# A two-layer diffusion backbone: where the first feed-forward's gate vectors are fetched and multiplied

## The chip, the cores and the metric

The kernel runs on one core of one Trainium2 chip. The metric is the device time of one execution in microseconds (us). A core has a matrix engine (TensorE, written PE in the profile; its weight loads are PEld), a vector engine (VectorE, DVE), a scalar engine (ScalarE, ACT), a general one (GpSimd, POOL) and SyncE (SP), which here only issues DMAs. Matrix products are written to PSUM, which the kernel splits into eight banks of 128 x 512 floats: four "g", three "m" and one "v".

## What is computed

The reference runs two layers over 256 latent and 256 context tokens of width 1024. Layer 0 has a mixer of two kinds of scanned heads (GLA and mLSTM), layer 1 a Mamba-2 mixer; each is followed by a feed-forward with a depthwise convolution. Each half of a layer is modulated by vectors made from the conditioning vector `c` (and `c_ctx` for the context tokens):

```python
mod_l = (jax.nn.silu(c) @ mod_w[layer] + mod_b[layer])[:, None, :]
sh1l, sc1l, g1l, sh2l, sc2l, g2l = jnp.split(mod_l, 6, axis=-1)
...
xl = xl + g1l * yl                                   # the mixer's residual
hl = modulate(xl, norm_ffn_g[layer], sh2l, sc2l)     # norm, scale, shift
xl = xl + g2l * conv_ffn(hl, ...)                    # the feed-forward's residual
```

The products with `mod_w` (1024 x 6144 for each layer) have two useful rows each, but 25 MB of weights per layer. The last of the six vectors, `g2`, is the gate of the feed-forward.

## The kernel before

All activations lie transposed: `xT[k]` holds 128 features by 512 tokens (256 context, then 256 latent). Weights come from HBM in raw tiles of 1 MB (16 blocks of 128 x 128), and each half tile is split into a rounded part `wh` (ACT, L173) and a rest `wl` (DVE or POOL, L174), so that three fast matmuls (L185 to L187, helper `mm3`) replace one exact one. `Stream` does this one unit of eight blocks ahead; raw tiles lie in two buffers of the pool `rawp` (the feed-forward's up weights in two of their own, `ur`), split ones in four.

A product with `mod_w` is cut in chunks of 512 columns. `mod_chunk(l, j)` makes chunk j (0 to 11) of layer l: it loads 2 MB, runs eight exact fp32 matmuls (16 records on L244; four at a time lie side by side in the array, each 32 columns wide), copies the result to SBUF (ACT, L261), transposes it (PE, L264) and sums and biases it into `comps[l][j // 2]` (DVE, L268 to L272, helper `mod_out`). Chunks 10 and 11 are the gate `g2`, which layer 0 uses first in the feed-forward's residual. Chunk (1, 2) is half of the scale that layer 1's first norm uses.

Chunks run as fillers in other work. `Stream` has a list `fill`; whenever it loads a new raw tile it takes one element and calls it. `fill1[:-1]` is given to the first feed-forward's up weights from raw tile 2 on, so that each further tile takes a chunk; these use the pool `rawp` for their weights and the single "v" bank (`vps`) for result and transposes. The down weights of that feed-forward use `rawp`, too.

The order around the change in the program text: in `even_mixer` the four mLSTM heads (`head(0)` to `head(3)`), the output gates (`gates`), then `finish(0)` to `finish(3)`, each of which normalizes a head and writes two operands of the out-projection (`hh`, `hl`; square on ACT at L729, transposes L737, rounding L738, rest L739). Chunk (0, 10) stands ahead of `finish(0)` and chunk (0, 11) ahead of `finish(3)`; their weights use the four buffers "b4" of the mixer's pool `sp`, in loads of 512 KB. The out-projection follows: four column blocks at once, then four one after the other, each with its residual (L334) and a square that is summed for the norm (L286, L288; `Norm.add`). The norm: column sums by PE (L132), a reciprocal root in small DVE operations (L112 to L123), a spread over the partitions by four PE transposes (L140), a copy (L141), then for each of eight tiles DVE (L315), ACT (L321) and DVE (L323). Chunk (1, 2) stands between the spread and these tiles. The feed-forward (`conv_ffn`) makes up products for pairs j of column blocks (`project(j)`), convolves them on DVE (L798) and multiplies them down in two halves of 11 pairs. In the last pair of a half, `project(10)`, the second product goes to the "v" bank.

Program order is not the order on an engine. The tile framework plans each engine's queue ahead of time from estimated durations, and places waits by tile: so out-projection matmuls stand between those of the heads, and a chunk's matmuls between those of other products. Buffers of one name are given out in turn as they come free.

Of the kernel before, what the change touches and what calls it, by code (L numbers as in the profile page):

```python
# [9 lines left out]
F32 = mybir.dt.float32  # L10
# [6 lines left out]
P = 128  # L17
D = 1024
KD = 8
# [32 lines left out]
def block_kernel(ctx: ExitStack, tc: tile.TileContext, A: dict, out: bass.AP):  # L52
    nc = tc.nc
    PSUM = bass.MemoryType.PSUM
    v, s, g, te = nc.vector, nc.scalar, nc.gpsimd, nc.tensor
# [8 lines left out]
    rawp = ctx.enter_context(tc.tile_pool(name="rawp", bufs=2))  # L64
# [9 lines left out]
    def nm(b):  # L74
        _u[0] += 1
        return f"{b}_{_u[0]}"
# [149 lines left out]
    spad = cp.tile([P, KD, 32], F32, tag="spad", name="spad")  # L226
# [5 lines left out]
    ident = load(A["ident"], [P, P])  # L232
    comps = [[cp.tile([P, KD, 2], F32, tag=f"mod{l}_{i}", name=f"mod{l}_{i}") for i in range(6)] for l in range(2)]

    def mod_chunk(l, j, pool=rawp, psa=vps, tag="raw", n=2, bufs=None):

        ps = psa()
        w = KD // n
        for i in range(n):
            raw = pool.tile([P, w * 512], F32, tag=tag, name=nm("rawm"), bufs=bufs)  # L240
            nc.sync.dma_start(out=raw, in_=A["modw"][l, j, :, i * w * 512:(i + 1) * w * 512])
            for kk in range(w):
                k = i * w + kk
                te.matmul(out=ps[32 * (k % 4):32 * (k % 4) + 32, :], lhsT=spad[:, k, :], rhs=raw[:, kk * 512:(kk + 1) * 512],  # L244
                          start=k < 4, stop=k >= 4)
        mod_out(l, 4 * j, 4, ps, psa)

    def mod_part(q, pool, psa):

# [8 lines left out]
    def mod_out(l, c, n, ps, psa):  # L258

        ev = t2((P, n * P))  # L260
        s.copy(out=ev, in_=ps)  # L261
        pt = psa()[:, :n * P].rearrange("p (a b) -> p a b", b=P)
        for a in range(n):
            te.transpose(pt[:, a, :], ev[:, a * P:(a + 1) * P], ident)  # L264
        col = lambda name, o: pc(name, o, n).unsqueeze(2).to_broadcast([P, n, 2])
        i, k = c // KD, c % KD
        dst = comps[l][i][:, k:k + n, :]
        v.tensor_reduce(out=dst, in_=pt.rearrange("p a (q c) -> p a c q", q=4)[:, :, 0:2, :], axis=AX.X, op=ALU.add)  # L268
        v.tensor_tensor(out=dst, in0=dst, in1=col("modb", l * 48 + c), op=ALU.add)
        if i in (1, 4):  # L270

            v.scalar_tensor_tensor(out=dst, in0=dst, scalar=1.0, in1=col("nmg" if i == 1 else "nfg", l * 8 + k), op0=ALU.add, op1=ALU.mult)  # L272
# [33 lines left out]
    def norm_mod(l, comp_sh, comp_sc, segs, r, between=lambda k, acts: None, tiles=None):  # L306
        c0, c1 = segs[0][1], segs[-1][2]
        hs = [] if tiles is None else tiles
        sh, sc = comps[l][comp_sh], comps[l][comp_sc]
        acts = lambda k: hs[k]  # L310
        for k in range(KD):
            between(k, acts)
            y = t2()
            for ci, a, b in segs:
                v.scalar_tensor_tensor(out=y[:, a:b], in0=xT[k][:, a:b], scalar=sc[:, k, ci:ci + 1], in1=r[:, a - c0:b - c0],  # L315
                                       op0=ALU.mult, op1=ALU.mult)
            if tiles is None:
                hs.append(htiles(k))
            h_, l_ = hs[k]
            for ci, a, b in segs:  # L320
                s.activation(out=h_[:, a:b], in_=y[:, a:b], func=AF.Identity, bias=sh[:, k, ci:ci + 1])  # L321
            for ci, a, b in segs:
                v.scalar_tensor_tensor(out=l_[:, a:b], in0=y[:, a:b], scalar=sh[:, k, ci:ci + 1], in1=h_[:, a:b].bitcast(F32),  # L323
                                       op0=ALU.add, op1=ALU.subtract)
        return acts
# [18 lines left out]
    E = Ctx()  # L344
# [11 lines left out]
    with tc.tile_pool(name="stp", bufs=6) as stp:  # L356
        warm(10, ones)
        nrm = Norm(0, T)
# [17 lines left out]

        acts = norm_mod(0, 0, 1, SEGS, r, start)
    fill0 = [lambda j=j: mod_chunk(0, j) for j in (4, 5, 8, 9, 6, 7)]
    fill1 = [lambda j=j: mod_chunk(1, j) for j in (3, 0, 1, 4, 5, 8, 9, 6, 7, 11)]
    E.fill0, E.W0 = fill0, W0  # L380
    nrm = Norm(0, T)
    with ExitStack() as st:
        even_mixer(E, st, acts, pss0, nrm.add)
    for k in range(KD):
        dump(f"x1_{k}", xT[k])
    r = nrm.row()
    mod_chunk(1, 2, rawp, mps)
    acts = norm_mod(0, 3, 4, SEGS, r)
    with ExitStack() as st:
        hs, nrms = [], [Norm(a, b) for _, a, b in SEGS]  # L390

        def then(m, sgs):
            for sg in sgs:
                nrms[sg[0]].add(m)
                if m == KD - 1:
                    hs[:] = hs or [htiles(k) for k in range(KD)]
                    norm_mod(1, 0, 1, (sg,), nrms[sg[0]].row(), tiles=hs)

        conv_ffn(E, st, acts, fill1[:-1], then)
# [14 lines left out]
def even_mixer(E, st, acts, pss0, then):  # L414
# [343 lines left out]
    head(2)  # L758
    head(3)
    gates()  # L760
    E.mod_chunk(0, 10, sp, E.vps, "b4", 4, 4)
    finish(0)
    finish(1)
    finish(2)
    E.mod_chunk(0, 11, sp, E.vps, "b4", 4, 4)
    finish(3)
    for k in range(8):
        dump(f"m{k}", hh[k].bitcast(F32))
    WO = E.Stream(A["wout0"], 64)
# [4 lines left out]
    for m in range(4, KD):  # L774
        E.residual(0, 2, m, E.gemm_f(WO, 8 * m, KD, oa), SEGS)
        then(m)


class Conv:
# [586 lines left out]
```

## Time and profile before

| | |
|---|---|
| median of three runs | 1285.78 us (1279.78, 1285.78, 1286.11) |
| the profiled execution | 1282.09 us, of which the span of its instructions 1280.3 us |
| busy: PE, DVE, ACT, POOL | 96%, 72%, 46%, 33% of the span |
| chain that ended last | PE 75%, DVE 10%, issue 4%, DMA 4%, ACT 4%, POOL 2% |
| mean granted TensorE clock | 0.987 of full speed |
| L244, the chunks' matmuls | vps x288 and mps x32 records (20 chunks of 16) |

How to read it: a busy share is an average over stages with different limits. The chain is followed back from the last instruction, at each step to what released it. In a timeline a row has the start in us, the time it took, engine, line, operation, the tile written and the tiles read, and how many instructions of one kind in a row it stands for; in brackets the idle time of that engine before it and what ended it. Matmuls are pipelined: the time that one costs is the distance from start to start, not its duration. Tile names are the program's, with the buffer number left out.

### The profile page before, as it was taken

To read this page: it belongs to the slowest core of one execution; us is meant where nothing else is said; L and a number is where in the kernel's file an instruction comes from. 1 tells how busy PE (TensorE), PEld (TensorE's weight loads), DVE (VectorE), ACT (ScalarE), POOL (GpSimd) and SP (SyncE) were. 2 spreads that over 40 slices of the span, in tenths; PEclk is the share of its full clock that TensorE was granted. 3 is DMA by queue.
4 is the path that set the end of the run, shared out by engine and by line. 5 is a ranking of instruction groups with operands and counts; after the bars stand their busy time and mean duration, and the time that the engine had idled before them with its cause. 6 is when DMAs were issued, how large, how long until landed. Compare 5 with 4: busy or idle time off the path is not lost.

```text
span 1280.3 us, 18746 instructions
## 1 busy us (share of the span) xinstructions
PE 1227.8 (96%) x7094; PEld 1003.9 (78%) x7094; DVE 926.0 (72%) x2061; ACT 594.4 (46%) x937; POOL 428.8 (33%) x249
## 2 busy tenths in 40 slices
PE   7989999999999999999999999999999998999995
PEld 5657787876867777888888897888888897899994
DVE  4483889487658776227785478888888956989995
ACT  4463345344344333223443346666666645555543
POOL 0100000000225565326666000032222224999974
PEclk8999999999999999999999999999999998999998
DMA  9557202334536564222211225453544376555521
GB/s 372 200 187 234 107 22 78 129 107 165 172 130 263 202 259 166 99 99 99 99 66 66 99 75 147 142 168 124 165 131 125 108 270 218 193 172 191 178 91 61
DMA packets 40106, 191.45 MB, mean 150 GB/s; under 512 B 4608, under 2 KB 10568, under 8 KB 21072
## 3 DMA queue, kind: packets, MB, share of 16 engines
q1 hardware_dynamic: 36512, 185.48, 41.6%
q10 hardware_dynamic: 3504, 4.77, 1.2%
q8 instruction: 56, 0.92, 0.3%
q14 instruction: 34, 0.28, 0.1%
HBM read 189.03 MB, written 1.20 MB: 149 GB/s over the span
## 4 chain that ended last, share of the span: by engine, by line
PE 75%; DVE 10%; issue 4%; DMA 4%; ACT 4%; POOL 2%; SPq 0%; DVEq 0%; ACTq 0%; POOLq 0%
PE gps L185 12%; PE gps L186 12%; PE gps L187 12%; PE mps L185 6%; PE mps L187 6%; PE mps L186 6%; PE vps L244 3%; PE gps L932 1%; PE vps L1174 1%; PE gps L933 1%; PE gps L931 1%; POOL wl L174 1%; PE gps L220 1%; PE gps L222 1%; PE gps L221 1%
## 5 line engine op out<-in xcount | busy, mean ns | idle before, releaser
L174 POOL TENSOR_TENSOR wl<-raw,wh 128x1024 fp32r<-128x1024 f32 x122 | 293.6, 2415 | 495.7 <-ACT wh L173 459.4
L173 ACT ACTIVATE wh<-raw 128x1024 fp32r<-128x1024 f32 x226 | 237.4, 1054 | 170.8 <-PE gps L187 99.6
L185 PE MATMUL gps<-hh,wh 128*128 128x512 f32 (+1 forms) x824 | 290.8, 354 | 6.7 <-ACT hh L321 4.9
L186 PE MATMUL gps<-hh,wl 128*128 128x512 f32 (+1 forms) x824 | 289.6, 352 | 1.1 <-DVE wl L174 1.1
L187 PE MATMUL gps<-hl,wh 128*128 128x512 f32 (+1 forms) x824 | 290.2, 353 | 0.0
L798 DVE SCALAR_TENSOR_TENSOR y<-mps,fcw,y 128x255 f32<-128x255 f32 (+3 forms) x592 | 247.5, 433 | 51.7 <-ACT y L792 37.5
L185 PEld LDWEIGHTS gps<-hh,wh 128*128 128x128 f32 x824 | 155.6, 189 | 41.7 <-issue 12.5
L174 DVE TENSOR_TENSOR wl<-raw,wh 128x1024 fp32r<-128x1024 f32 x104 | 127.6, 1234 | 79.6 <-ACT wh L173 79.4
L185 PE MATMUL mps<-hh,wh 128*128 128x256 f32 (+1 forms) x544 | 178.2, 328 | 0.0
L187 PE MATMUL mps<-hl,wh 128*128 128x256 f32 (+1 forms) x544 | 176.5, 325 | 1.6 <-DVE hl L323 1.6
L186 PE MATMUL mps<-hh,wl 128*128 128x256 f32 (+1 forms) x544 | 177.0, 325 | 0.0
L186 PEld LDWEIGHTS gps<-hh,wl 128*128 128x128 f32 x824 | 156.1, 189 | 23.2 <-issue 3.2
L187 PEld LDWEIGHTS gps<-hl,wh 128*128 128x128 f32 x824 | 156.0, 190 | 20.8 <-issue 1.7
L185 PEld LDWEIGHTS mps<-hh,wh 128*128 128x128 f32 x544 | 105.4, 194 | 16.9 <-issue 6.7
L187 PEld LDWEIGHTS mps<-hl,wh 128*128 128x128 f32 x544 | 105.2, 194 | 9.2 <-DVE hl L323 1.8
L186 PEld LDWEIGHTS mps<-hh,wl 128*128 128x128 f32 x544 | 105.6, 194 | 7.8
L798 DVE SCALAR_TENSOR_TENSOR y<-gps,fcw,y 128x189 f32<-128x189 f32 (+3 forms) x180 | 77.7, 438 | 22.0 <-ACT y L792 18.2
L792 ACT ACTIVATE y<-mps,fcw 128x256 f32<-128x256 f32 (+1 forms) x68 | 41.2, 637 | 91.5 <-PE mps L187 91.5
L185 PE MATMUL gps<-mh,wh 128*128 128x512 f32 (+1 forms) x198 | 73.5, 371 | 0.0
L187 PE MATMUL gps<-ml,wh 128*128 128x512 f32 (+1 forms) x198 | 73.4, 371 | 0.0
L186 PE MATMUL gps<-mh,wl 128*128 128x512 f32 (+1 forms) x198 | 73.4, 370 | 0.0
L334 DVE SCALAR_TENSOR_TENSOR x<-gps,mod,x 128x256 f32<-128x256 f32 x56 | 24.2, 478 | 42.0 <-PE gps L187 42.0
(292 smaller groups left out, 1894.0 us busy)
## 6 DMA issues: line engine op xcount, KB each, us to landing
raw<-in_up SPq DMA_DIRECT2D x42, 1024.0 KB, 4.9
rawm<-in_modw SPq DMA_DIRECT2D x36, 1024.0 KB, 6.6
raw<-in_win SPq DMA_DIRECT2D x32, 1024.0 KB, 5.4
raw<-in_dn SPq DMA_DIRECT2D x20, 1024.0 KB, 5.1
raw<-in_wout SPq DMA_DIRECT2D x10, 1024.0 KB, 5.6
rawm<-in_mods SPq DMA_DIRECT2D x8, 1024.0 KB, 14.5
R<-crd SPq DMA_DIRECT2D x32, 256.0 KB, 4.2
rawm<-in_modw SPq DMA_DIRECT2D x8, 512.0 KB, 5.0
```

Source lines behind the costliest of these rows:

```text
L173: s.activation(out=hi[:, :n], in_=rw, func=AF.Copy)
L174: self.eng(u).tensor_tensor(out=lo[:, :n], in0=rw, in1=hi[:, :n].bitcast(F32), op=ALU.subtract)
L185: te.matmul(out=ps, lhsT=lhi, rhs=rhi, start=first, stop=False)
L186: te.matmul(out=ps, lhsT=llo, rhs=rhi, start=False, stop=False)
L187: te.matmul(out=ps, lhsT=lhi, rhs=rlo, start=False, stop=last)
L220: te.matmul(out=ps, lhsT=ah[:, sl], rhs=hi[:, c:c + 512], start=k == 0, stop=False)
L221: te.matmul(out=ps, lhsT=ah[:, sl], rhs=lo[:, c:c + 512], start=False, stop=False)
L222: te.matmul(out=ps, lhsT=al[:, sl], rhs=hi[:, c:c + 512], start=False, stop=k == nk - 1)
L244: te.matmul(out=ps[32 * (k % 4):32 * (k % 4) + 32, :], lhsT=spad[:, k, :], rhs=raw[:, kk * 512:(kk + 1) * 512], start=k < 4, stop=k >= 4)
L334: v.scalar_tensor_tensor(out=xT[m][:, a:b], in0=ps[:, a - base:b - base], scalar=gt[:, m, ci:ci + 1], in1=xT[m][:, a:b], op0=ALU.mult, op1 ...
L792: self.E.s.activation(out=y, in_=ps, func=AF.Identity, scale=self.fcw[:, c + 4:c + 5], bias=self.fcw[:, c + 9:c + 10])
L798: self.E.v.scalar_tensor_tensor(out=o, in0=i, scalar=self.fcw[:, ti * 10 + wi:ti * 10 + wi + 1], in1=o, op0=ALU.mult, op1=ALU.add)
```

## The change

Chunks (0, 10) and (0, 11) are no longer made among the `finish` calls. `mod_chunk` is split into `mod_load` (buffers and DMAs), `mod_go` (matmuls) and the old `mod_out`. The loads now stand behind `finish(3)`, ahead of the out-projection's: (0, 10) in the four "b4" buffers as before, (0, 11) in the two "tok" buffers in which the mixer held its values, with 1 MB each. The matmuls stand behind the out-projection, in "g" banks; (0, 10) is finished there, while the copy, transposes and sums of (0, 11) are returned as a function and called behind `norm_mod`. Chunk (1, 2) leaves the norm and becomes the first element of `fill1`, all others move back by one.

```diff
--- before.py
+++ after.py
@@ -232,18 +232,25 @@
     ident = load(A["ident"], [P, P])
     comps = [[cp.tile([P, KD, 2], F32, tag=f"mod{l}_{i}", name=f"mod{l}_{i}") for i in range(6)] for l in range(2)]
 
+    def mod_load(l, j, pool=rawp, tag="raw", n=2, bufs=None):
+
+        w = KD // n * 512
+        for i in range(n):
+            raw = pool.tile([P, w], F32, tag=tag, name=nm("rawm"), bufs=bufs)
+            nc.sync.dma_start(out=raw, in_=A["modw"][l, j, :, i * w:(i + 1) * w])
+            yield raw
+
+    def mod_go(l, j, raws, psa):
+        ps = psa()
+        k = 0
+        for raw in raws:
+            for c in range(0, raw.shape[-1], 512):
+                te.matmul(out=ps[32 * (k % 4):32 * (k % 4) + 32, :], lhsT=spad[:, k, :], rhs=raw[:, c:c + 512], start=k < 4, stop=k >= 4)
+                k += 1
+        return lambda: mod_out(l, 4 * j, 4, ps, psa)
+
     def mod_chunk(l, j, pool=rawp, psa=vps, tag="raw", n=2, bufs=None):
-
-        ps = psa()
-        w = KD // n
-        for i in range(n):
-            raw = pool.tile([P, w * 512], F32, tag=tag, name=nm("rawm"), bufs=bufs)
-            nc.sync.dma_start(out=raw, in_=A["modw"][l, j, :, i * w * 512:(i + 1) * w * 512])
-            for kk in range(w):
-                k = i * w + kk
-                te.matmul(out=ps[32 * (k % 4):32 * (k % 4) + 32, :], lhsT=spad[:, k, :], rhs=raw[:, kk * 512:(kk + 1) * 512],
-                          start=k < 4, stop=k >= 4)
-        mod_out(l, 4 * j, 4, ps, psa)
+        mod_go(l, j, mod_load(l, j, pool, tag, n, bufs), psa)()
 
     def mod_part(q, pool, psa):
 
@@ -376,16 +383,16 @@
 
         acts = norm_mod(0, 0, 1, SEGS, r, start)
     fill0 = [lambda j=j: mod_chunk(0, j) for j in (4, 5, 8, 9, 6, 7)]
-    fill1 = [lambda j=j: mod_chunk(1, j) for j in (3, 0, 1, 4, 5, 8, 9, 6, 7, 11)]
+    fill1 = [lambda j=j: mod_chunk(1, j) for j in (2, 3, 0, 1, 4, 5, 8, 9, 6, 7, 11)]
     E.fill0, E.W0 = fill0, W0
     nrm = Norm(0, T)
     with ExitStack() as st:
-        even_mixer(E, st, acts, pss0, nrm.add)
+        rest = even_mixer(E, st, acts, pss0, nrm.add)
     for k in range(KD):
         dump(f"x1_{k}", xT[k])
     r = nrm.row()
-    mod_chunk(1, 2, rawp, mps)
     acts = norm_mod(0, 3, 4, SEGS, r)
+    rest()
     with ExitStack() as st:
         hs, nrms = [], [Norm(a, b) for _, a, b in SEGS]
 
@@ -758,12 +765,16 @@
     head(2)
     head(3)
     gates()
-    E.mod_chunk(0, 10, sp, E.vps, "b4", 4, 4)
     finish(0)
     finish(1)
     finish(2)
-    E.mod_chunk(0, 11, sp, E.vps, "b4", 4, 4)
     finish(3)
+
+    mods = [list(E.mod_load(0, 10, sp, "b4", 4, 4)), []]
+    for i in range(2):
+        raw = T_([P, 4, 516], "tok", bufs=2).rearrange("p a b -> p (a b)")[:, :2048]
+        nc.sync.dma_start(out=raw, in_=A["modw"][0, 11, :, i * 2048:(i + 1) * 2048])
+        mods[1].append(raw)
     for k in range(8):
         dump(f"m{k}", hh[k].bitcast(F32))
     WO = E.Stream(A["wout0"], 64)
@@ -774,6 +785,8 @@
     for m in range(4, KD):
         E.residual(0, 2, m, E.gemm_f(WO, 8 * m, KD, oa), SEGS)
         then(m)
+    E.mod_go(0, 10, mods[0], E.gps)()
+    return E.mod_go(0, 11, mods[1], E.gps)
 
 
 class Conv:
```

## Rows read from the trace of the kernel before

**Rows 1.** Busy us by stage: length, PE, PEld, DVE, ACT, POOL, clock, DMA

```profile
296.00:353.00 57.00, 55.85 (x270) 41.44 (x269) 38.63 (x99) 18.88 (x30) 7.25 (x3) 1.00 0.49 170
353.00:362.00 9.00, 6.22 (x43) 3.35 (x41) 5.07 (x21) 3.76 (x7) 2.36 (x1) 1.00 0.46 168
362.00:400.00 38.00, 38.00 (x178) 28.44 (x179) 25.39 (x61) 18.64 (x29) 12.99 (x6) 0.96 0.49 191
```

**Rows 2.** Timeline of PE at the mixer's end

```profile
296.30 1.06 PE L244 MATMUL vps<-rawm,spad 128*32 128x512 f32 x8
297.30 0.50 PE L185 MATMUL gps<-hh,wh 128*128 128x512 f32 x1
...
300.19 1.05 PE L244 MATMUL vps<-rawm,spad 128*32 128x512 f32 x4
302.40 1.05 PE L244 MATMUL vps<-rawm,spad 128*32 128x512 f32 x4 [1.15 <-DMA rawm<-in_modw]
...
304.41 0.60 PE L264 MATMUL vps<-c,t 128*128 128x128 f32 x4
304.77 0.48 PE L185 MATMUL gps<-hh,wh 128*128 128x512 f32 x1
```

**Rows 3.** Timeline of ACT, DVE and PE around finish(3)

```profile
312.84 0.62 ACT L729 ACTIVATE t<-qk 128x512 f32<-128x512 f32 x1
...
321.13 0.75 DVE L739 SCALAR_TENSOR_TENSOR hl<-mps,c,hh 128x512 fp32r<-128x512 f32 x1 [1.48 <-ACT hh L738]
...
328.63 0.39 PE L185 MATMUL gps<-hh,wh 128*128 128x512 f32 x1
```

**Rows 4.** Timeline of PE and DVE through the norm

```profile
352.89 0.39 PE L187 MATMUL gps<-hl,wh 128*128 128x512 f32 x1
...
354.10 1.04 PE L244 MATMUL mps<-rawm,spad 128*32 128x512 f32 x2
...
356.16 1.92 PE L244 MATMUL mps<-rawm,spad 128*32 128x512 f32 x14
...
358.51 0.16 DVE L123 SCALAR_TENSOR_TENSOR ry<-rw,ry 128x4 f32<-128x4 f32 x1
...
358.83 0.55 PE L264 MATMUL mps<-c,t 128*128 128x128 f32 x3 [0.75 <-ACT t L261]
359.21 0.60 PE L140 MATMUL vps<-c,ry 128*128 128x128 f32 x4
...
361.95 0.53 PE L185 MATMUL gps<-hh,wh 128*128 128x512 f32 x1 [2.03 <-ACT hh L321]
```

**Rows 5.** Busy us by stage: one stretch behind the norm

```profile
364.00:365.00 1.00, 1.00 (x4) 0.81 (x3) 1.00 (x4) 0.72 (x2) 0.00 (x0) 0.50 1.06 451
```

**Rows 6.** Timeline of PE, one chunk in the feed-forward

```profile
380.10 1.92 PE L244 MATMUL vps<-rawm,spad 128*32 128x512 f32 x16
```

**Rows 7.** Timeline around the last chunk and the down-projection's start

```profile
487.86 1.92 PE L244 MATMUL vps<-rawm,spad 128*32 128x512 f32 x16
...
488.98 0.33 SPq L159 DMA_DIRECT2D raw<-in_dn  x1
...
491.63 0.19 DVE L268 TENSOR_REDUCE mod<-vps 128x8 f32<-128x32 f32 x1
...
501.23 0.39 PE L185 MATMUL vps<-hh,wh 128*128 128x512 f32 x1
...
506.67 0.40 PE L185 MATMUL gps<-mh,wh 128*128 128x512 f32 x1
...
507.75 4.61 DVE L798 SCALAR_TENSOR_TENSOR y<-vps,fcw,y 128x255 f32<-128x255 f32 x10 [0.82 <-ACT y L792]
```

**Rows 8.** Page, groups (busy us, mean ns of one); DMA issues (us to landing)

```profile
L174 POOL TENSOR_TENSOR wl<-raw,wh 128x1024 fp32r<-128x1024 f32 x122 | 293.6, 2415 | 495.7 <-ACT wh L173 459.4
L173 ACT ACTIVATE wh<-raw 128x1024 fp32r<-128x1024 f32 x226 | 237.4, 1054 | 170.8 <-PE gps L187 99.6
...
raw<-in_dn SPq DMA_DIRECT2D x4, 512.0 KB, 5.8
```

## The prediction, made before the change was run

> **What bounds the kernel now.** I read the chain that ended last first (mostly TensorE, PE), then the table by stage, which says where PE is the limit [rows 1]: between 296 and 353 us (end of the first mixer, out-projection) PE is busy 55.85 of 57.00 us, in the feed-forward's first 38 us all 38, but in the 9 us between (the norm) only 6.22. So in the first and third stretch every PE instruction that is removed or added counts at its full price, as long as its operands are there; in the norm PE waits for a chain over VectorE (DVE) and ScalarE (ACT), and work put there is free as long as it doesn't stand in front of that chain. The change moves three products of one kind between these stages. I call them fills: 0/10 and 0/11 (gates of the first feed-forward) and 1/2 (a scale of the second layer). Last I read the timeline around each of them.
>
> **Part A: 0/10 and 0/11 leave the mixer's end.** A fill is 16 PE records on L244 and 4 transposes on L264. Fill 0/10 took PE from 296.30 to 297.30 (8 records), and from 300.19 to 303.40 (4 records, an idle 1.15 us for the weights, 4 records from 302.40, 1.0 us) [rows 2]: 1.00 + 3.21 us. Fill 0/11 comes in three such pieces without the wait, 3.0 us. The four transposes of each delay the next matmul from 304.41 to 304.77, 0.36 us. Sum: 4.21 + 3.00 + 0.72 = 7.9 us. It is all gained if the out-projection's matmuls can close up, and they can if their operands are ready. The last one, hl of finish(3), was ready at 321.13 + 0.75 = 321.88, and its twelve matmuls began at 328.63 [rows 3], 6.75 us of slack. If finish(3) didn't move at all, the gain would be 6.7 us, not 7.9. But it will move: its square waited until 312.84 [rows 3], on an ACT queue that also held the evacuations of both fills. I take 7.4 us (bounds 6.7 and 7.9).
>
> The eight loads of these weights become six and stay where they are in SP's queue; those of 0/11 now need "tok" buffers, free after the last head. The out-projection's last load stands behind them as before. I cost this at nothing: that load's blocks are used in the last quarter of the out-projection. If that cover were gone, the price would be one landing, about 6 us.
>
> **Part B: the norm.** The last out-projection matmul starts at 352.89 and the first feed-forward matmul at 361.95 [rows 4], 9.06 us. Now PE does fill 1/2 there; later it does 0/10 and 0/11. Fill 1/2 hardly cost anything: PE is in it until 356.16 + 1.92 = 358.08, and the chain (the reciprocal root on DVE) ends at 358.51 + 0.16 = 358.67. Only three of its transposes, which had waited for their ACT copy, stand ahead of the four that spread the root over the partitions; these start at 359.21 instead of 358.7, 0.5 us late. Two fills need 2 x (1.92 + 0.36) = 4.6 us of PE. There are 0.75 us idle before 358.83, 2.1 us idle between the spread's end (359.81) and 361.95, and the 2.4 us that 1/2 gives back: 5.3 us. It fits, if the order is right. Bounds: with all 32 records and the first four transposes ahead of the spread, PE comes to it at 356.16 + 30 x 0.12 + 0.55 = 360.3 [rows 4], 1.1 us later than now; two copies and small DVE operations of mod_out ahead of the chain's could add 0.9: +2.0 us. Below nothing: the spread 0.5 us early, and the clock. [...] Before it fell, PE had been idle for 2.1 us. If the second fill closes this, the clock may hold: -2.0 us in all. I take +0.3 us, nearest to the row of 1/2, which cost 0.5.
>
> [...] The rows show that the spread's transposes started 0.5 us after their operand, behind three that waited for a copy. [...]
>
> **Part C: 1/2 becomes a fill of the feed-forward.** fill1 gets one more element, so ten fills instead of nine run there, each in its turn. One costs 1.92 us [rows 6] and 0.36 us of transposes, 2.3 us of a full PE. And the last of them comes to another place. A fill is taken with every 16th block of the up weights; the tenth meets project(10), whose second product goes into the one vps bank (from 501.23) [rows 7], where fills are done too. The ninth held that bank from 487.86 until DVE had reduced it at 491.63 + 0.19, 4.0 us; so project(10)'s second half waits up to 4.0 - 2.3 = 1.7 us. The tenth also holds both "raw" buffers until it is multiplied, from 501.2 to 502.2 for the first. The down-projection's first load was issued at 488.98, right behind the ninth fill [rows 7]; now it goes at 502.3. Landing 5.8, ACT's rounding 1.05, GpSimd's rest 2.4 us [rows 8]: 511.6 us. The down-projection began at 506.67 [rows 7]; its new due time is 506.67 + 2.3 + 1.7 = 510.7, so 0.9 us are lost there. C lies between 2.3 us (the tenth is multiplied as soon as it lands, before its turn) and 2.3 + 1.7 + 0.9 = 4.9 us. I take 3.4, near the middle, as no row shows a fill in this place.
>
> **Sum.** -7.4 + 0.3 + 3.4 = -3.7 us. The profiled execution took 1282.09 us (span 1280.3); the change would make that 1278.4. The median of the three runs is 3.69 us (0.29%) higher, 1285.78, so the forecast stands at 1282.1. The bounds together are -7.9 - 2.0 + 2.3 = -7.6 and -6.7 + 2.0 + 4.9 = +0.2 us: 1278.2 to 1286.0.
>
> **Rivals.**
> 1. Both fills stand before the spread. For it: all of 1/2's records and three transposes did. Against: they were all that PE had to do. -7.4 + 2.0 + 3.4 = -2.0 us, 1283.8.
> 2. Faster: the clock holds through the norm, the spread loses its 0.5 us, the tenth fill is multiplied early. For it: PE's longest idle time in the norm gets work. Against: the clock fell in spite of 4 us of L244 shortly before. -7.6 us, 1278.2.
> 3. Slower: the tenth fill loses the vps bank. If project(10)'s second half takes the bank first, the fill waits until DVE has convolved that product, 507.75 + 4.61 = 512.4 us [rows 7]. Both raw buffers stay full, the down-projection's load goes at 513.4 and is split at 513.4 + 5.8 + 1.05 + 2.4 = 522.7, while PE has nothing else from 506.67 on: 16 us, and 0.5 us of the fill that isn't covered. It decides from the point where the fill's weights land later than project(10)'s first half ends, or where the planner ranks the product first. Against: the ninth's fill went ahead of its product. -7.4 + 0.3 + 16.5 = +9.4 us, 1295.2.
> 4. The weights of 0/10 and 0/11 now live until the norm, in space that the first up weights may be meant for. Then these wait for the fills, some 6 us after the last out-projection matmul; 9.25 us of landing and splitting [rows 8] make 15.3 instead of 9.06: B is +6.2, the sum +2.2 us, 1288.0. Against: the mixer frees far more space than these 33 KB of each partition.
> 5. The change doesn't do what it says: the planner multiplies both fills inside the out-projection, at 4.6 us of a full PE, and the norm gets its 0.5 us back. -7.4 + 4.6 - 0.5 + 3.4 = +0.1 us, 1285.9. Against: 1/2, which depends on nothing in the out-projection, began at 354.10, behind its last matmul [rows 4].
>
> **How the numbers follow.** Forecast 52%, rival 1 14%, rival 2 15%, rival 3 8%, rival 4 4%, rival 5 7%. The predicted time is the forecast's, 1282 us. The range must take in 1278.2 to 1286.0; the three runs shown differ by 6.3 us, so I widen it to 1276 and 1289, which leaves out rival 3 and a few per cent of the others. A measurement of this kernel can tell about 0.5% (6.4 us) from no change. Faster by more than that: rival 2 and the lower edge of the forecast, 0.23. Slower: rival 3 and the upper edge of rival 4, 0.10. Within: 0.67.
>
> **What would show it.** A: no L244 between 290 and 315, no idle time of PE there, and the last out-projection matmul at about 345.5. B: 32 records of L244 right behind it; from that matmul to the first of the feed-forward 9 us again (7 to 11); the clock 1.00 behind it, or not. C: ten fills after the norm, the last before or within project(10); the idle time ahead of the first down-projection matmul says which bound holds. The prediction is wrong if PE has gaps in the out-projection (then operands, not PE, were the limit), or if the down-projection starts more than 3 us behind project(10).

## The result, and the profile after

The changed kernel takes 1298.01 us (median of 4 runs), the kernel before in the same comparison 1282.97 us: a ratio of 1.0103 with a 95% interval of 1.0078 to 1.0129. By the ratio it is 13 us slower (by the medians 15) where 4 us faster were forecast, and outside the predicted range.

Where the time went can be read from the starts of the same VectorE instructions in the two profiled runs (1296.84 against 1282.09 us). After minus before:

| stretch of the kernel before | shift in it | forecast |
|---|---|---|
| up to 250 us | +0.7 | 0 |
| 250 to 262 us, mLSTM heads | +3.5 | 0 |
| 290 to 348 us, mixer's end (part A) | -8.9 | -7.4 |
| 348 to 440 us, norm and start of the feed-forward (part B) | +15.1 | +0.3 |
| 500 to 520 us, last fills (part C) | +3.9 | +3.4 |
| the rest | +0.3 | 0 |

A and C came with the forecast sign, each somewhat larger. Two stretches carry the error: B, and one in the heads of which the prediction had said nothing. First the table by stage (stretch, its length, busy time of each engine, granted clock, DMA share and rate):

```profile
core 0: us, PE busy (x) PEld busy (x) DVE busy (x) ACT busy (x) POOL busy (x), PEclk, DMA share, GB/s
296.00:347.00 51.00, 51.00 (x249) 42.32 (x248) 33.32 (x102) 17.56 (x32) 0.00 (x0) 1.00 0.32 113
347.00:357.00 10.00, 9.25 (x63) 4.65 (x61) 3.20 (x16) 1.22 (x2) 0.00 (x0) 1.00 0.01 2
357.00:385.00 28.00, 18.02 (x64) 12.53 (x64) 19.27 (x34) 12.38 (x23) 13.96 (x4) 0.76 0.56 207
```

The mixer's end is closed up: 51 of 51 us busy, against 55.85 of 57 [rows 1]. But in the 28 us behind the norm TensorE works for only 18, at a mean clock of 0.76; before, it was full there at 0.96 [rows 1]. GpSimd, idle until 357, works half of this time. TensorE's timeline through the norm:

```profile
348.27 1.05 PE L132 MATMUL vps<-ones,acc 128*128 128x128 f32 x8
351.32 1.92 PE L248 MATMUL gps<-rawm,spad 128*32 128x512 f32 x14
354.57 1.92 PE L248 MATMUL gps<-tok,spad 128*32 128x512 f32 x16
356.43 0.65 PE L140 MATMUL vps<-c,ry 128*128 128x128 f32 x4
357.75 1.92 PE L248 MATMUL vps<-rawm,spad 128*32 128x512 f32 x16 [0.67 <-ACT rstd L141]
362.62 0.92 PE L185 MATMUL mps<-hh,wh 128*128 128x512 f32 x2 [2.94 <-ACT wh L173]
365.12 0.80 PE L186 MATMUL mps<-hh,wl 128*128 128x512 f32 x1 [1.57 <-POOL wl L174]
377.64 0.80 PE L186 MATMUL mps<-hh,wl 128*128 128x512 f32 x1 [4.79 <-POOL wl L174]
```

Both fills (on L248 in this kernel) stand ahead of the spread (L140, at 356.43; the last out-projection matmul began at 348.04, so 8.38 us behind it, against 6.33 before [rows 4]); this is rival 1. Behind them even 1/2 is multiplied, first of the ten. Then TensorE waits for the up weights, which it did not do there before ([rows 4] show only a wait for hh): for wh from ScalarE, and twice for wl from GpSimd. SyncE's queue tells why they are late, in its timeline and in its list of waits (in total, times, longest):

```profile
356.56 0.33 SPq L159 DMA_DIRECT2D raw<-in_up  x1
```
```profile
SPq L159 <- PE gps L248: 25.6, 1, 25.6
```

The up weights' first load was issued at 356.56, right behind the last matmul of 0/11, after waiting 25.6 us for it; before, it was issued at 320.51. That is rival 4's wait. Its landing and the split of the weights (ScalarE's rounding and GpSimd's subtraction), which had been done inside the out-projection, now lie in and behind the norm (ACT and POOL, then two rows of the table by stage):

```profile
361.51 1.06 ACT L173 ACTIVATE wh<-raw 128x1024 fp32r<-128x1024 f32 x1 [1.95 <-DMA raw<-in_up]
362.70 4.88 POOL L174 TENSOR_TENSOR wl<-raw,wh 128x1024 fp32r<-128x1024 f32 x2 [310.92 <-DMA raw<-in_up]
371.02 9.09 POOL L174 TENSOR_TENSOR wl<-raw,wh 128x1024 fp32r<-128x1024 f32 x2 [3.44 <-ACT wh L173]
```
```profile
373.00:378.00 5.00, 0.36 (x1) 0.36 (x2) 4.87 (x8) 2.98 (x6) 5.00 (x2) 0.87 0.00 0
378.00:383.00 5.00, 5.00 (x15) 3.93 (x15) 0.00 (x0) 0.00 (x0) 2.10 (x1) 0.50 0.36 106
```

The third subtraction, from 371.02 to the matmul that it lets go at 377.64, took 6.6 us; one takes 2.4 us elsewhere [rows 8]. Behind the idle time that it makes, the clock is 0.50 for 5 us. (It is at 0.50 from 363 to 368 too, behind the wait for wh.)

The second loss, in the heads. SyncE's and VectorE's timelines, and the table by stage:

```profile
246.93 0.33 SPq L776 DMA_DIRECT2D tok<-in_modw  x1
```
```profile
254.47 0.35 DVE L705 SCALAR_TENSOR_TENSOR b<-b,RQT,c_trineg 128x128 f32<-128x128 f32 x1 [2.89 <-DMA b<-prd]
```
```profile
246.00:250.00 4.00, 3.61 (x25) 3.04 (x24) 3.52 (x15) 0.60 (x1) 0.00 (x0) 1.00 0.76 244
250.00:254.00 4.00, 4.00 (x20) 3.24 (x18) 1.58 (x8) 1.85 (x3) 0.00 (x0) 1.00 0.65 250
254.00:258.00 4.00, 1.71 (x10) 1.29 (x9) 3.53 (x10) 1.96 (x3) 0.00 (x0) 0.90 0.00 0
258.00:262.00 4.00, 4.00 (x14) 3.25 (x13) 3.06 (x7) 1.17 (x4) 0.00 (x0) 0.68 0.38 131
```

The first half of 0/11 is loaded at 246.93 already: one of the two "tok" buffers is free as soon as the linear attention has read gv. While this 1 MB arrives (250 GB/s), VectorE waits 2.89 us for the broadcast of a head's gates on ScalarE's queue; TensorE runs dry (busy 1.71 of 4 us), and its clock falls to 0.68 in the 4 us behind that.

### The profile page after: what moved, and what is told of

Its sections match the earlier page's. It is cut to its first block, busy times and chain, and to the rows that moved or that the text cites. A ratio compares the mean times of both kernels' runs of the same rounds, so it can differ in the third digit from the quotient of the medians.

```text
span 1294.7 us, 18744 instructions
## 1 busy us (share of the span) xinstructions
PE 1231.0 (95%) x7094; PEld 1007.9 (78%) x7094; DVE 924.1 (71%) x2061; ACT 594.2 (46%) x937; POOL 433.1 (33%) x249
## 4 chain that ended last, share of the span: by engine, by line
PE 72%; DVE 13%; issue 5%; DMA 4%; ACT 3%; POOL 2%; SPq 0%; DVEq 0%; POOLq 0%; ACTq 0%
PE gps L185 12%; PE gps L186 12%; PE gps L187 12%; PE mps L185 6%; PE mps L186 6%; PE mps L187 6%; DVE y L811 2%; PE vps L248 2%; PE gps L945 1%; PE vps L1187 1%; PE gps L946 1%; PE gps L944 1%; PE mps L721 1%; POOL wl L174 1%; DMA rawm<-in_modw 1%
## 5 line engine op out<-in xcount | busy, mean ns | idle before, releaser
L174 POOL TENSOR_TENSOR wl<-raw,wh 128x1024 fp32r<-128x1024 f32 x122 | 298.0, 2452 | 497.3 <-DMA raw<-in_up 310.9
L805 ACT ACTIVATE y<-mps,fcw 128x256 f32<-128x256 f32 (+1 forms) x68 | 41.2, 636 | 91.3 <-PE mps L187 91.3
```

Source lines behind the costliest of these rows:

```text
L174: self.eng(u).tensor_tensor(out=lo[:, :n], in0=rw, in1=hi[:, :n].bitcast(F32), op=ALU.subtract)
L805: self.E.s.activation(out=y, in_=ps, func=AF.Identity, scale=self.fcw[:, c + 4:c + 5], bias=self.fcw[:, c + 9:c + 10])
```

## The experiments

Four questions: is it the late load that makes B, or the fills ahead of the spread and the clock? What makes the load late? Is it the load of 0/11 that delays the heads? Does C stand alone? To compare the norm across runs I count from the start of the last out-projection matmul, in us: the issue of the up weights' first load, the spread, the feed-forward's first matmul, and its 96th (by then the late weights have made themselves felt).

| kernel | median us | ratio (95%) | up load | spread | first | 96th |
|---|---|---|---|---|---|---|
| before | 1282.97 | | -32.4 | 6.33 | 9.06 | 34.9 |
| changed | 1298.01 | 1.0103 (1.0078-1.0129) | 8.5 | 8.38 | 14.57 | 49.3 |
| own_tiles | 1293.16 | 1.0098 (1.0076-1.012) | -17.3 | 8.38 | 12.51 | 48.6 |
| late_release | 1290.64 | 1.006 (1.0042-1.0077) | 1.5 | 7.56 | 13.24 | 41.2 |
| later_release | 1290.0 | 1.0039 (1.0022-1.0057) | 8.1 | 6.32 | 14.11 | 41.2 |
| vector_split | 1292.1 | 1.0067 (1.0044-1.0089) | 8.5 | 8.38 | 14.68 | 47.9 |
| up_first | 1280.55 | 0.9975 (0.9956-0.9995) | -30.9 | 8.38 | 11.54 | 35.5 |
| three_mended | 1275.41 | 0.9935 (0.9913-0.9957) | -28.3 | 8.38 | 11.54 | 38.0 |
| spread_first | 1279.08 | 0.9945 (0.9926-0.9963) | -28.3 | 5.93 | 11.61 | 39.4 |

(Each ratio is to runs of the kernel before on the same chip. Ahead of the 96th matmul lie two fills in the kernel before and in the two release kernels, four in three_mended and spread_first, three in the others; a fill costs 2.3 us where TensorE is full, 1.92 [rows 6] and 0.36 [rows 2]. A difference of 1 us or so between two kernels at the 96th matmul tells nothing: load_after_heads, below, has the norm of the changed kernel unaltered and comes to 47.9 instead of 49.3; fills_earlier, below, has the norm of the kernel before and comes to 36.1 instead of 34.9. In both pairs the granted clock was at 0.50 for a different time (5 us in the changed kernel, where load_after_heads has a mean of 0.74; 3 us in the kernel before, 5 us in fills_earlier). Nor do whole times carry small differences: behind 530 us, where no run changes anything, the profiled executions still shift by -3.6 to +4.5 us against the one before. So I read each effect from its own stretch.)

**own_tiles: the changed kernel, the new pools waiting tile by tile.**

```diff
-        self.fp = st.enter_context(E.tc.tile_pool(name="fp", bufs=1))
+        self.fp = st.enter_context(E.tc.tile_pool(name="fp", bufs=1, reuse_waits="pool" if l else "tile"))
-    ur = st.enter_context(E.tc.tile_pool(name="ur", bufs=2))
+    ur = st.enter_context(E.tc.tile_pool(name="ur", bufs=2, reuse_waits="tile"))
```

> The changed kernel, with one thing undone: the pools of the feed-forward's up weights and convolution table no longer wait for every user of the mixer's closed pools, but each of their tiles only for earlier tiles on its own bytes. Theory 1 (the norm grew by 15.2 us because the up weights' first load waits until the fills 0/10 and 0/11, the last users of the mixer's pools, are multiplied; it was issued at 356.56 against 320.51 before): the first up load is issued near 320 again, the first feed-forward matmul starts 7 to 10 us after the last out-projection matmul, and the time is 11 us (9 to 14) under the changed kernel's, about 1287. Theory 2 (the growth comes from 32 matmuls ahead of the root's spread and from the clock of TensorE behind them): the load comes early, the time falls by 0 to 3 us only.

The load came early, at 328.54, so it had waited for a pool and not for bytes. Yet the stretch from 348 to 440 us still grew by 14.5 us: theory 1 as I had put it fell. The timelines of SyncE, ScalarE, GpSimd, TensorE and VectorE, a row by stage, and a row of SyncE's list of waits show what is left:

```profile
328.54 0.42 SPq L159 DMA_DIRECT2D raw<-in_up  x1
351.05 0.33 SPq L159 DMA_DIRECT2D raw<-in_up  x1
354.88 0.58 ACT L141 COPY rstd<-vps 128x512 f32<-128x512 f32 x1 [3.18 <-PE vps L140]
357.23 1.04 ACT L173 ACTIVATE wh<-raw 128x1024 fp32r<-128x1024 f32 x1
358.35 18.52 POOL L174 TENSOR_TENSOR wl<-raw,wh 128x1024 fp32r<-128x1024 f32 x4 [307.51 <-ACT wh L173]
369.71 0.79 PE L186 MATMUL mps<-hh,wl 128*128 128x512 f32 x1 [10.66 <-POOL wl L174]
367.38 2.56 DVE L330 SCALAR_TENSOR_TENSOR hl<-t,mod,hh 128x256 fp32r<-128x256 f32 x1
```
```profile
358.00:369.70 11.70, 0.73 (x2) 0.30 (x2) 11.70 (x25) 9.69 (x19) 11.35 (x2) 0.65 0.20 81
```
```profile
SPq L159 <- PE gps L248: 21.5, 1, 21.5
```

ScalarE idles 3.18 us for the spread and rounds the weights only behind it, though their load had been issued 28.7 us before: its order is written when the kernel is built, and the split stands behind the spread in it. (Why the planner put it there is not shown.) GpSimd's first subtraction then starts at 358.35, and the matmul that needs it goes on at 369.71, after 11.3 us. VectorE is busy all that time (11.70 of 11.70 us) with the norm's operations, two operands each; GpSimd gets through only at the end of that chain, where VectorE's last one takes 2.56 us instead of 0.48. So early loads alone are no use: what costs is that the split falls into the norm. Nor did this run free all of them: the second up tile's load (351.05) still waited 21.5 us for the matmuls of fill 0/10, on whose bytes that tile lies.

**late_release and later_release: the kernel before, only the release is late.**

```diff
+    te.matmul(out=E.gps()[:, 0:1], lhsT=tri[:, :P], rhs=E.xT[7][:, 0:1], start=True, stop=True)
```

This stands behind the out-projection in late_release. In later_release it reads the norm's row instead of xT[7], inside the mixer's pools.

> The kernel before, plus one matmul of a single column behind the out-projection, which reads the mask table of the mixer's pool and whose product nobody reads. It costs TensorE some 0.1 us, and that table's bytes are used by no up weight. Theory 1 (a new pool waits for every user of the closed pools on whose bytes it lies): the up weights' first load goes from 320.5 to about 354, the norm grows by 9 to 14 us, and so does the time, to about 1294, without any fill moved. Theory 2 (only the 32 matmuls in the norm and the clock cost time): 0, 1283. A third (a tile waits only for earlier tiles on its own bytes): 0 as well.

> The kernel before, plus the one matmul of a single column as in late_release, but its other operand is the norm's result, so that the mixer's pool is read last behind the norm's spread, some 8 us behind the last out-projection matmul (in the changed kernel 8.5, in late_release 1.5). Nothing else moves. Counted from the last out-projection matmul to the 96th of the feed-forward: 34.9 us before, 41.2 in late_release, 49.3 in the changed kernel, 35.5 in up_first. Theory 1 (only the moment of the release counts; every us that it comes later costs about one): 34.9 + 6.3 + 6.5 = 47.7 us (46 to 49), the time about 1296. Theory 2 (a late release costs a fixed 6.3 us, and the other 8 of the changed kernel are made by the fills): 41 to 42 us, the time about 1290.

One matmul of a column, which reads bytes that no up weight uses, moves the load from 32 us ahead of the last out-projection matmul to 1.5 us behind it, and costs 6.3 us by the 96th matmul: rival 4's mechanism, with no fill moved. But 6.6 us later still it costs the same 6.3 us: theory 1 of later_release fell, and its rival held. The two runs pay in different places. ScalarE in late_release, then in later_release:

```profile
360.14 0.37 ACTq L788 DMA_DIRECT2D fcw<-in_fcw  x1
360.61 0.63 ACT L286 ACTIVATE t<-x 128x512 f32<-128x512 f32 x1 [5.31 <-DVE most L292]
367.27 0.57 ACT L141 COPY rstd<-vps 128x512 f32<-128x512 f32 x1
```
```profile
364.06 0.58 ACT L141 COPY rstd<-vps 128x512 f32<-128x512 f32 x1 [1.07 <-PE vps L140]
370.10 1.06 ACT L173 ACTIVATE wh<-raw 128x1024 fp32r<-128x1024 f32 x1 [2.86 <-DMA raw<-in_up]
```

In the first the convolution table's load, which waits for the same release, sits on ScalarE's queue ahead of the norm's last square, and two roundings ahead of the copy of the spread; in the second the norm runs on time and the weights come 6 us behind it. (Their whole times hold something else too: in their profiles 0/10 waited 4.2 and 2.7 us for its weights, against 1.15 [rows 2], and the mixer's end was 5.4 and 4.3 us longer than in the kernel before, ahead of anything that these runs change. The fill that the change removes has a wait that varies.)

**vector_split: the changed kernel, the first four subtractions on VectorE.**

```diff
-    up = E.Stream(E.A["up0"], 44 * KD, fill, 1, 2, pool=ur, eng=lambda u: g)
+    up = E.Stream(E.A["up0"], 44 * KD, fill, 1, 2, pool=ur, eng=lambda u: v if u < 4 else g)
```

> The changed kernel, with the second half of the split (weights less their rounded part) of the first four up units on VectorE instead of GpSimd; the loads come as late as in the changed kernel. [...] If only the late landing counts, VectorE's chain gets 4.9 us longer and the time stays or goes up by up to 3 us.

TensorE and VectorE in the norm:

```profile
361.43 0.73 PE L185 MATMUL mps<-hh,wh 128*128 128x512 f32 x2 [3.05 <-ACT wh L173]
369.70 1.12 PE L271 MATMUL gps<-c,t 128*128 128x128 f32 x4 [7.53 <-ACT t L268]
370.13 1.22 DVE L174 TENSOR_TENSOR wl<-raw,wh 128x1024 fp32r<-128x1024 f32 x1
```

The waits for GpSimd (1.57 and 4.79 us in the changed kernel) are gone, but the four subtractions, at 1.2 us each, now stand at the end of VectorE's chain of the norm (the first at 370.13, though its weights were rounded by 361.4), and TensorE idles 7.53 us instead. The stretch from 348 to 440 us grew by 13.7 us, and the 96th matmul came at 47.9: both as in load_after_heads, where the norm is the changed kernel's. So no gain in the norm is shown. The median is 5.9 us under the changed kernel's, but the intervals of the two ratios overlap. That a subtraction took 6.6 us in the changed kernel and 11.3 in own_tiles, beside VectorE's chain, is seen; to take it off GpSimd doesn't help as long as the split lies there.

**up_first: the changed kernel at other addresses.**

```diff
+    tk = st.enter_context(tc.tile_pool(name="tk", bufs=2))
     sp = st.enter_context(tc.tile_pool(name="sp", bufs=2))
...
+    ur = st.enter_context(E.tc.tile_pool(name="ur", bufs=2))
     cv = Conv(E, st, 0, T)
-    ur = st.enter_context(E.tc.tile_pool(name="ur", bufs=2))
```

(The three "tok" tiles go to tk.)

> The changed kernel with the same operations, but other addresses: the up weights' pool comes first in the space that the mixer frees, and the tiles of 0/11 get a pool of their own, so that no byte of the up weights' pool belongs to a pool that holds weights of 0/10 or 0/11. Theory 1 (the norm grew by 15.1 us mainly because the up weights' pool waits for the two fills, so that loads, ScalarE's rounding and GpSimd's subtraction all fall into the norm, where the subtraction comes into VectorE's chain of two-operand operations and takes up to 11 us instead of 2.4): the first four subtractions run within the out-projection again at 2.4 us each, the growth falls to 2 to 5 us (the fills ahead of the root's spread remain), and the time is 10 to 13 us under the changed kernel's 1298, about 1286. Theory 2 (the fills ahead of the spread and TensorE's clock make most of it): 0 to 4 us less, 1294 to 1298.

SyncE, GpSimd and TensorE, and the stretch behind the norm:

```profile
315.82 0.33 SPq L159 DMA_DIRECT2D raw<-in_up  x1
332.04 2.39 POOL L174 TENSOR_TENSOR wl<-raw,wh 128x1024 fp32r<-128x1024 f32 x1 [281.01 <-ACT wh L173]
348.31 2.36 POOL L174 TENSOR_TENSOR wl<-raw,wh 128x1024 fp32r<-128x1024 f32 x1 [3.05 <-ACT wh L173]
355.07 0.65 PE L140 MATMUL vps<-c,ry 128*128 128x128 f32 x4
```
```profile
357.00:385.00 28.00, 28.00 (x132) 21.14 (x124) 16.64 (x46) 15.54 (x26) 7.76 (x4) 1.00 0.33 114
```

The four subtractions are back inside the out-projection at 2.4 us each, and B is +1.4 us instead of +15.1 (from -6.2 to -4.8 in VectorE's starts). With the same operations and the same order of the fills, 13.7 us hang on which addresses the up weights get: theory 1, and by more than it had expected. The fills ahead of the spread cost 2.5 us at the first matmul (11.54 against 9.06), but TensorE is now full behind it and its clock stays at 1.00, where it was 0.50 before [rows 5]; by the 96th matmul 0.6 us are left, though TensorE has by then done one fill more than before.

**load_after_heads: the changed kernel, 0/11 held until the last head.**

```diff
+        if i == 0:
+            v.tensor_copy(out=raw[:, 0:1], in_=hm[3][:, 0, 0:1])
         nc.sync.dma_start(out=raw, in_=A["modw"][0, 11, :, i * 2048:(i + 1) * 2048])
```

> The changed kernel, with the first half of the weights of 0/11 loaded only behind the last mLSTM head (a copy of one column of that head's result into the tile holds it). Theory 1 (the 1 MB load that now starts at 246.93 shares the DMA engines with the heads' broadcast loads and so costs 3.5 us around 250 to 262): DVE's wait of 2.89 us for the broadcast disappears, and the time is 3.5 us (2.5 to 4.5) under the changed kernel's. Theory 2 (the heads are late for another reason, as another order of instructions on an engine): 0. If the load is needed earlier than it now lands, the time goes up: it has 50 us, so not expected.

```profile
250.00:254.00 4.00, 4.00 (x19) 3.31 (x18) 2.83 (x13) 1.46 (x3) 0.00 (x0) 1.00 0.27 89
254.00:258.00 4.00, 3.44 (x19) 2.58 (x18) 4.00 (x13) 3.26 (x5) 0.00 (x0) 1.00 0.08 24
```

The heads' shift is +0.2 us instead of +3.5; the clock stays at 1.00. Over the whole run it is 1292.2 us (1.0073, 1.0056 to 1.0089), 5.8 under the changed kernel's median where 3.5 were expected; the ratios differ by 3.9 us and their intervals overlap. The stretch itself gave 3.3. In the norm, which is unaltered, 1.4 us came back as well: GpSimd's third subtraction takes 6.6 us as before, but the clock in the 5 us behind it is 0.74 instead of 0.50. With the load left early the heads' shift was 3.6 us in own_tiles, 2.1 in vector_split and 1.8 in up_first, so its size varies; no run shows on what it depends.

**ten_fills: the kernel before, only 1/2 moved.**

```diff
-    fill1 = [lambda j=j: mod_chunk(1, j) for j in (3, 0, 1, 4, 5, 8, 9, 6, 7, 11)]
+    fill1 = [lambda j=j: mod_chunk(1, j) for j in (2, 3, 0, 1, 4, 5, 8, 9, 6, 7, 11)]
...
-    mod_chunk(1, 2, rawp, mps)
```

> The kernel before with only the third part of the change: product 1/2 leaves the norm and becomes the first of ten fills of the feed-forward; 0/10 and 0/11 stay as they were. Theory 1 (the tenth fill costs its own 2.3 us of a full TensorE and holds the vps bank and both raw buffers, so that the down-projection starts late): +3.4 us (2.3 to 4.9) between 480 and 520 us, and the norm 0 to 0.5 us shorter. Theory 2 (what the changed kernel lost at 500 to 520 us is another thing's doing, and the tenth fill is hidden in the norm, where it is multiplied anyway): 0, within 1 us.

SyncE and TensorE in ten_fills:

```profile
503.13 0.33 SPq L159 DMA_DIRECT2D raw<-in_dn  x1
505.72 0.50 PE L185 MATMUL vps<-hh,wh 128*128 128x512 f32 x1 [0.28 <-DVE mod L268]
```

+3.94 us between 500 and 520 us, the same as in the changed kernel, and -0.15 in the norm: C stands alone, at 3.9. The median is 4.3 us up (1.0027, 1.0005 to 1.0048); the profiled execution itself only 1.0, as its starts fall back by 3.6 us behind 530 us.

**fills_earlier: the kernel before, 0/10 and 0/11 in the mixer's input projection.**

```diff
-    fill0 = [lambda j=j: mod_chunk(0, j) for j in (4, 5, 8, 9, 6, 7)]
+    fill0 = [lambda j=j: mod_chunk(0, j) for j in (4, 5, 8, 9, 6, 7, 10, 11)]
...
-    E.mod_chunk(0, 10, sp, E.vps, "b4", 4, 4)
-    E.mod_chunk(0, 11, sp, E.vps, "b4", 4, 4)
```

> The kernel before, with 0/10 and 0/11 as seventh and eighth fill of the mixer's input projection (their weights through the raw buffers, as the six before them), and nothing else. If the stretch from 296 to 353 us is bound by TensorE and by the wait for these weights, it is 8.9 us shorter, as in every run of the changed kernel; the linear attention's stretch, where TensorE waits for other engines, takes up the two products at 0 to 2 us: 1274 to 1276. If the fills, their copies on ScalarE or the raw buffers they hold are in the way there, 3 to 6 us come back: 1277 to 1280.

The mixer's end is 8.9 us shorter, as in every kernel that takes these two fills out of it; but in and behind the linear attention some 3.5 us came back: the starts are 1.8 us early at 176 us, 3.5 us late at 232 and 1.7 late at 290. That is the second of the two cases expected. 1277.46 us against 1284.88: 0.9942 (0.9918 to 0.9965).

**three_mended and spread_first.** three_mended joins up_first and load_after_heads, and starts the feed-forward's fills one load earlier:

```diff
-    up = E.Stream(E.A["up0"], 44 * KD, fill, 1, 2, pool=ur, eng=lambda u: g)
+    up = E.Stream(E.A["up0"], 44 * KD, fill, 1, 1, pool=ur, eng=lambda u: g)
```

> The changed kernel with all three found losses taken back: the up weights' pool apart from the fills' weights (as up_first), 0/11's load held until the last head's result, and the feed-forward's fills from its second load on instead of its third, so that the tenth comes where the ninth came before. From the parts: 1283 - 8.9 (mixer's end) + 0 (heads) + 2 to 3 (fills ahead of the spread) + 0 to 1 (tenth fill) = 1276 to 1278. If the losses overlap or another wait takes their place, it stays above 1280.

It is faster than both kernels, 0.65% under the one before: 1275.41 us, 0.9935 (0.9913 to 0.9957). The shift between 500 and 520 us is 0, and the down-projection's first load is out at 482.96, ahead of project(10):

```profile
482.96 0.33 SPq L159 DMA_DIRECT2D raw<-in_dn  x1
```

spread_first is three_mended with both fills queued behind the spread (an issue order on TensorE behind its last transpose; the lines that keep this transpose are left out here):

```diff
+        r = nrm.row()
+        with tc.issue_after(spun[0].ins):
+            rest = [f() for f in rest]
```

> As three_mended, with both fills queued behind the four transposes that spread the root instead of ahead of them. In every run of the changed kind the spread came 8.38 us behind the last out-projection matmul against 6.33 before, and in up_first the first feed-forward matmul 11.54 us behind it against 9.06. If it is the fills' place that costs these 2.05 us, the spread is back at 5.9 to 6.4 us; the fills then run while VectorE makes the first operands, 3.9 us, of which 2.1 are idle anyway, so the first matmul comes at 10.5 to 11.5 us: 0 to 1 us under three_mended's 1275.4. If the idle time that this order leaves ahead of the spread lets TensorE's clock fall again (0.50 in the kernel before, 1.00 in up_first), 1.5 us are lost: 1275 to 1277.

The spread is early again, at 5.93 us, but the first matmul at 11.61, where it was: the fills then stand ahead of it instead. And the clock falls, as the expectation had allowed:

```profile
345.00:354.00 9.00, 5.51 (x36) 3.01 (x38) 4.92 (x19) 3.39 (x6) 2.35 (x1) 0.81 0.35 118
```

TensorE idled 2.65 us ahead of the spread, and the first fill behind it took 2.85 us from start to start where the second took 1.82. The stretch from 348 to 440 us is 1.4 us longer than in three_mended. Nothing is gained (0.9945, 0.9926 to 0.9963, an interval that overlaps three_mended's).

## Why the prediction was wrong, step by step

**Part B, the step that failed.** "Against: the mixer frees far more space than these 33 KB of each partition": with this sentence rival 4 got 4 in 100, and the forecast's +0.3 for B took the first up weights as loaded and split by the time of the norm, as they were before. That was the wrong wait: their first load was issued 36 us later, and B was +15.1. The amount of space is not the question. In the built program the convolution table lies at bytes 136416 to 138176 of a partition and the first up tile at 195520 to 203712; the weights of 0/11 lie at 174176 to 190688 and those of 0/10 at 209632 to 226016. Neither overlaps (the second up tile, at 203712 to 211904, does overlap 0/10's), and both loads waited all the same: here a new pool waited for all users of every closed pool whose bytes it touches. own_tiles and up_first show it from both sides (first load at 328.54 and 315.82, against 356.56). The kernel before has the same wait, in SyncE's list of waits, which I had ahead of the prediction and did not read this way:

```profile
SPq L159 <- DVE qk L733: 14.6, 1, 14.6
```

The up load issued at 320.51 had waited 14.6 us for the last normalization of finish(3) (L733, at 318.97), the mixer's last work on tiles of these pools, and the change makes the fills that last work.

**Rival 4's price.** It said 6.2 us, from a landing and a split behind the release. The two runs that hold the release and nothing else gave 6.3, but this nearness is luck: by rival 4's sum, 9.25 us behind the release, late_release (released at 1.5) should have lost 1.7 us and later_release (at 8.1) 8.2; their first matmuls came 11.8 and 6.1 us behind the release. And the changed kernel paid 14.4 by the 96th matmul at the same release as later_release. Its traces differ in three places: the spread 2.05 us late, 4.8 us of waiting for GpSimd's third subtraction (6.6 us long, against 3.5 at the same place of later_release), and a second stretch of 5 us at a clock of 0.50 behind that, 2.5 us by estimate, 0.50 x 5 (later_release has one such stretch, the changed kernel two). These add up to 9.3 of which 8.1 show, and the two kernels also differ by one fill; I have not parted them by a run. What rival 4 lacked is that the split shares the norm with VectorE's chain: it took GpSimd's 2.4 us [rows 8] as fixed, and the subtraction took 6.6 here and 11.3 in own_tiles.

**Rivals 1 and 2 came true together.** The "+2.0 us" of rival 1's bound was measured as 2.05 at the spread, in every kernel of the changed kind but spread_first. The size is in part luck: the bound's last 0.9 us was for copies and small VectorE operations ahead of the chain's, but the chain was done at 353.57, 2.9 us ahead of the spread; it was TensorE that waited, 0.75 us for ScalarE's copy ahead of the transposes of 0/10:

```profile
353.99 0.66 PE L271 MATMUL gps<-c,t 128*128 128x128 f32 x4 [0.75 <-ACT t L268]
```

And in up_first, where no wait for weights hides it, the clock held, at 1.00 from 357 to 385 us. The 1.5 us for the clock in the prediction's lower bound for B, -2.0, are an estimate that no run shows; the traces show a mean clock of 0.96 over 38 us in the kernel before [rows 1], with its matmuls 0.43 us from start to start at 363.39 (clock 0.50) and 0.23 at 366.41 (clock 1.00), and in up_first 1.00 throughout. With that estimate the sum of the two rivals, +0.5, is near what up_first shows, 0.6 at the 96th matmul and 1.4 by 440 us. The spread went when its place in the order came: 8.38 us behind the last out-projection matmul with the fills ahead of it, 5.93 with the fills behind it (spread_first), where the work behind it paid instead (first matmul at 11.61 against 11.54).

**The load of 0/11, taken at nothing.** "those of 0/11 now need 'tok' buffers, free after the last head": that holds for one of the two. The other is free after the linear attention, so 1 MB went out 50 us earlier, into the heads. I had asked what stands behind these loads in SyncE's queue, not what an earlier load meets at the DMA engines. Price 3.5 us; load_after_heads takes 3.3 of it back.

**Part A was right in kind and too small.** -8.9 us in all eight kernels that take both fills out of the mixer's end, against -7.4 (6.7 to 7.9). From the starts in the trace before, the two fills' matmuls cover 1.00 + 3.19 + 2.96 us; each group of transposes costs 0.44, not 0.36 (the matmul behind it is 0.08 us late as well); and at each of the five pieces in which the fills ran, the start ahead and the start behind lie about 0.1 us further apart than elsewhere (305.31 to 305.64 and 306.64 to 306.97, against 0.23), 1.0 us in all, a term that the sum did not have. That makes 9.0. And finish(3) gave no resistance, as TensorE without a gap from 296 to 347 shows; the bound of 6.7 was never near. Where 0/10 waits longer for its weights, as in the two release runs, the gain would be larger.

**Part C was right within its bounds:** 3.9 against 3.4 (2.3 to 4.9), alone and in company. The fill's own 2.3 us and the term that I had put on the vps bank, 1.7 at most, make all of it (TensorE idles 0.85 us for the copy ahead of the transposes and 0.28 behind DVE). The third term, 0.9 for the late load, is not there: in ten_fills the first subtraction is done by 510.7 and the down-projection begins at 511.30 without a wait. So 3.4, a middle between bounds, was near by luck. The load's time was right: in the changed kernel it went at 512.70, 10.25 us of which are the shift up to there, so 502.45 against 502.3. Rivals 3 and 5 did not happen: the tenth fill had the vps bank (511.57) ahead of project(10)'s second product (515.28), and both other fills ran behind the out-projection.

**The sum.** Without the pool's wait the forecast was close: up_first, which still has 1.8 us of the early load's price, came to -3.2 us by its ratio (-5.7 to -0.6), where -3.7 had been forecast for the change. By its trace it is less close: A, B, C and the heads are -8.9, +1.4, +3.9 and +1.8 us, -1.8 together.

## What to carry to other kernels

When a read is moved later, ask which pool its operand lives in and which pool will be laid on that pool's bytes: the new pool's first loads, and everything that a static order places behind them, go with the last read, whatever the tile's own address. Pools that are to be filled early belong on bytes whose users end early; that took a few lines here and was worth 13.7 us. When a load gets a buffer that comes free earlier, look at what else is on the DMA engines at that moment, not only at the queue behind it.

## What the runs showed of the hardware

GpSimd and VectorE slowed each other, in both directions. In own_tiles' norm GpSimd's subtraction of 2.4 us took 11.3 us, while 22 VectorE instructions with two operands each started one behind the other. In the out-projection it is VectorE that was slowed (groups of VectorE's instructions in the out-projection, first ten_fills, where GpSimd splits there, then the changed kernel, where it doesn't):

```profile
L288 DVE TENSOR_TENSOR acc<-acc,t 128x512 f32<-128x512 f32 x6 | 9.6, 1600 | 2.4 <-ACT t L286 2.4
```
```profile
L295 DVE TENSOR_TENSOR acc<-acc,t 128x512 f32<-128x512 f32 x6 | 4.1, 690 | 2.2 <-ACT t L293 2.2
```

The same addition takes 1600 ns in the mean with GpSimd beside it and 690 without. In own_tiles GpSimd's subtraction, beside a chain without a break, ended with the chain, after 11.3 us, and not behind one of its instructions of 0.48 us.

The clock of TensorE held at 1.00 behind the norm where three fills had filled its idle time to less than 1 us at a time (up_first, 0.75 and 0.68), and fell to 0.50 where it had idled 2.03 us [rows 4, rows 5]. And while a 1 MB load was under way in the changed kernel, at 250 GB/s in all, VectorE waited 2.89 us for a broadcast on another queue; without that load at that time (load_after_heads) the stretch lost 0.2 us instead of 3.5.
